# Query tiles of a PEER layer as fp16 pairs, and an even split of the gated expert columns

## The chip, the cores and the metric

The kernel runs on one core of a Trainium2 chip. The metric is the device time of one execution in microseconds, lower is better; where several runs were made, their median counts. The profile shows one execution, taken by the hardware profiler. Its engines are TensorE (PE; its weight loads are PEld), VectorE (DVE), ScalarE (ACT), GpSimd (POOL) and SyncE (SP), which issues most DMAs. L12 is line 12 of the kernel before.

## The reference

One decoder layer on 256 tokens of width 1024. An attention mixer (eight sparse-attention heads and four differential heads) comes first; the change doesn't touch it. Behind it stands a PEER layer, which is what this case is about:

```python
h = rmsnorm(x, norm2_g[l]) * (1 + sc_f) + sh_f
x = x + g_f * peer_ffn(h, peer_wq[l], peer_sub_keys[l], peer_u[l], peer_v[l])
return rmsnorm(x, final_g)

# peer_ffn, per chunk xc of 128 tokens
q = (xc @ wq).reshape(PEER_CHUNK, PEER_HEADS, 2, PEER_QDIM // 2)
sub = jnp.einsum('thpd,pkd->thpk', q, sub_keys)
sv, si = lax.top_k(sub, PEER_TOPK)
cand = sv[:, :, 0, :, None] + sv[:, :, 1, None, :]      # and the expert numbers cidx alike
best, pos = lax.top_k(cand, PEER_TOPK)
eid = jnp.take_along_axis(cidx, pos, axis=-1)
g = jax.nn.softmax(best, axis=-1)
act = jax.nn.gelu(jnp.einsum('td,thkd->thk', xc, u[eid]))
return jnp.einsum('thk,thkd->td', g * act, v[eid])
```

There are 8 heads, two halves of the query with 128 sub-keys each, 16 best per head, and 128 x 128 = 16,384 experts with a row of 1024 in `peer_u` and one in `peer_v`. A query tile is 128 columns of `wq`: 16 of them, two for each head.

## The kernel before

All 16,384 experts are computed densely. An expert's number is i * 128 + j; an expert tile j holds the 128 experts of one j, one to a partition. The layer runs in two loops of 128 steps, and a gating matrix, zero for all experts that a token did not choose, lies between them.

**The u loop** (`u_step`, L814). Step j loads 512 KB of `peer_u`, splits it into an fp16 pair (a scaled high part and the remainder, `split16`, L788: one operation of ScalarE at L793 and one of VectorE at L794), and makes three products for each of eight blocks of 128 features (`mm3`, L88 to L91): high times high, high times low, low times high. The 24 matmuls of 128x128 by 128x256 add up in one PSUM bank of pool `pu` (tile `up`, three buffers). ScalarE writes the gelu of the sum (L834) into the stash `st`, as 256 tokens of step j. The pair lies in one buffer of pool `hl` (tiles `w_hi` for even and `w_lo` for odd j, three buffers each). Loads and splits of expert tiles are traced with high priority.

**The range checks.** fp16 has a small range, so each split leaves a sum in a column of `chk`, and the first of each kind one in `big`. At the end `all_fit` (L1151) makes a flag of them, and if a number did not fit, a second version of the whole layer (fp32 pairs, from L1193) runs and writes the output again. Otherwise it is skipped.

**The choice of experts** (`topk_gen`, L856) is a generator that the u loop advances by a few steps after each expert tile (L1042). Heads 0 and 1 have their four query tiles from an earlier place (`qe`, L737 to L766, in fp32). For the other six heads, each of the two steps `wq` (L860) loads a query tile (`wraw`, a pool of its own with three buffers; the load has high priority) and multiplies it in fp32 with the fp32 input `h2` (L865). Two steps `sub_scores` (L869) multiply by the sub-keys `sk` (L873) and take the top 16 of each half with VectorE (`top16`, L849); a fifth step takes the top 16 of the sums. Two rounds of 14 steps then turn the choice into one-hot indices `kT` and weights `gT`, one round for 128 tokens. Where the steps and the loop's pace meet is at L1042: every second j before j = 12, then 2, 2, 1 steps in turn before j = 30, then one.

**Gating** (`g_build`, `g_apply`, `g_all`, L963 to L1008). For a group of eight tokens VectorE builds a one-hot A of the 128 i (L972) and a weighted one-hot of the j columns as two fp16 parts (B, Bl, L972 and L979); TensorE multiplies them (L988, two matmuls for each token, as wide as the j columns), and VectorE multiplies the result into the stash (L992). There are 32 groups of tokens, and two halves of the columns j: the first half (HJ = 72 columns, `st0`) is gated while the u loop goes on, as soon as the choice is done; the second (56 columns, `st1`) during the v loop. `paced` spreads the 65 steps of a half evenly, over the u steps that are left or over the first HJ - 6 v steps. Where u steps with j < 72 fall into the first half's gating, the expert tile is gated in part on the spot (L829 to L832, L994).

**The v loop** (`outputs`, L1049). Step j splits a 512 KB tile of `peer_v` and the gated stash row (tile `wt`, three buffers), and makes 12 matmuls of 128x128 by 128x512 (L1077) into four PSUM banks. Once the first HJ steps are past, the stash `st0` is scratch for the end of the kernel: final gains, inputs x (`xc`, L1101), modulation sums (`tail_prep`, L1106), one of its 20 pieces after each v step.

**Order and queues.** Within each engine instructions run in order. That order is made when the program is built: by priority, and by what an estimate says is ready. SP's queue carries the weight loads; ScalarE's queue carries the sub-keys (L842) and the store of `h2` (L843); POOL's queue carries the scratch loads (L1099, L1102, L1129, L1134).

Of the kernel before, what the change touches and what calls it, by code (L numbers as in the profile page):

```python
# [57 lines left out]
def block_kernel(ctx: ExitStack, tc: tile.TileContext, I, out):  # L58
# [50 lines left out]
    hchk = keep.tile([P, KD], F32, name="hchk")  # L109
    big = keep.tile([P, 3 + KD], F32, name="big")  # L110

# [642 lines left out]
    for k in range(KD):  # L754
        t = nrm[:, k % 2]
        V.tensor_mul(t, x2g[:, k, 0:T], rstd2)
        S.activation(h2[:, k], t, AF.Identity, bias=mod[:, 24 + k:25 + k])
        S.activation(h16[0][:, k], t, AF.Identity, bias=shs[:, k:k + 1], scale=SH, accum_out=big[:, 3 + k:4 + k])
        V.scalar_tensor_tensor(h16[1][:, k], h2[:, k], SH, h16[0][:, k], ALU.mult, ALU.subtract,
                               accum_out=hchk[:, k:k + 1])  # L760
# [21 lines left out]
    chk = keep2.tile([P, NCHK], F32, name="chk")  # L782
    G.memset(chk[:, 0:3 * NJ], 0.0)
    G.tensor_copy(chk[:, 3 * NJ:], hchk)
    first_one = {}
    bad_flag = keep2.tile([1, 1], I32, name="bad_flag")

    def split16(src, hi, lo, scale, i):  # L788
        kw = {}
        if i < 2 * NJ and i // NJ not in first_one:  # L790
            first_one[i // NJ] = i
            kw = dict(accum_out=big[:, 1 + i // NJ:2 + i // NJ])
        S.activation(hi, src, AF.Copy, scale=scale, **kw)  # L793
        V.scalar_tensor_tensor(lo, src, scale, hi, ALU.mult, ALU.subtract, accum_out=chk[:, i:i + 1])  # L794

    def load_split16(src, scale, i):
        with tc.high_priority(offset=None):
            t = load(src)
# [6 lines left out]
    pu = ps_u.enter_context(tc.tile_pool(name="pu", bufs=3, space=PSUM, reuse_waits="tile"))  # L805
    tk_stack = ExitStack()
    tk = tk_stack.enter_context(tc.tile_pool(name="tk", bufs=2, reuse_waits="tile"))
    tk1 = tk_stack.enter_context(tc.tile_pool(name="tk1", bufs=1, reuse_waits="tile"))

    act_box, hr_box = [], []  # L810
# [24 lines left out]

    iota_i = tk1.tile([P, P], I32, name="iota_i")
    G.iota(iota_i, pattern=[[1, P]], base=0, channel_multiplier=0)
    G.tensor_copy(iota, iota_i)
    c15 = tk1.tile([P, PH * TK], U32, name="c15")
    G.memset(c15, 15)  # L840
    sk = tk1.tile([P, 2, P], F32, name="sk")
    nc.scalar.dma_start(sk, I["peer_sub_keys"])  # L842
    nc.scalar.dma_start(h2d, h2)  # L843
    sv = tk1.tile([P, 2, 2, PH, TK], F32, name="sv")
    si = tk1.tile([P, 2, 2, PH, TK], U32, name="si")
    best = tk1.tile([P, 2, PH, TK], F32, name="best")
    bpos = tk1.tile([P, 2, PH, TK], U32, name="bpos")

    def top16(vals, tmp, vout, iout):  # L849
# [5 lines left out]

    def topk_gen():  # L856
        for h in range(PH):
            qs = {p: qe[:, 2 * h + p] for p in range(2)} if h < 2 else {}

            def wq(p):  # L860
                with tc.high_priority(offset=None):
                    w = load(I["peer_wq"][2 * h + p], pool=tk, name="wraw", bufs=3)
                ps = pu.tile([P, T], F32, name="up")
                for k in range(KD):
                    PE.matmul(ps, w[:, k * P:(k + 1) * P], h2[:, k], start=k == 0, stop=k == KD - 1)  # L865
                qs[p] = tk.tile([P, T], F32, name="qT")
                S.copy(qs[p], ps)

# [10 lines left out]

            for f, p in ((wq, 0), (wq, 1), (sub_scores, 0), (sub_scores, 1))[2 if h < 2 else 0:]:  # L880
                f(p)
                yield
# [141 lines left out]

    tg = topk_gen()
    alive = True
    gg = None
    for j in range(NJ):
        if not alive and gg is None:
            tk_stack.close()  # L1030
            st1_pool = ctx.enter_context(tc.tile_pool(name="stash1", bufs=1))
            st.append(st1_pool.tile([P, NJ - HJ, T], F32, name="st1"))
            act_stack = ExitStack()
            act_box.append(act_stack.enter_context(tc.tile_pool(name="actp", bufs=2)))
            h2_stack.close()
            gp_stack = ExitStack()
            gp_box.append(gp_stack.enter_context(tc.tile_pool(name="gp", bufs=2, side="right", reuse_waits="tile")))
            gg, first = g_all(0), j + 3
        u_step(j, True)
        done_j[0] = j + 1  # L1040
        if alive:
            alive = pump(tg, j % 2 if j < 12 else (2, 2, 1)[j % 3] if j < 30 else 1)  # L1042
        elif j >= first:
            paced(gg, j - first, NJ - 4 - first)
    ps_u.close()
    act_stack.close()
    w_pool = ctx.enter_context(tc.tile_pool(name="wp", bufs=LAST))

    def outputs(half, gg):  # L1049

        inner = ExitStack()
        py = inner.enter_context(tc.tile_pool(name="py", bufs=1, space=PSUM))
        if not half:
# [38 lines left out]
        def scratch(i, n=1):  # L1092
            return scr[:, i * D:(i + n) * D]
# [6 lines left out]
        xf = [scratch(4), scratch(5)]  # L1100
        xc = scratch(16, 2).rearrange("p (k t) -> p k t", k=KD)  # L1101
        nc.gpsimd.dma_start(xc, x2d)  # L1102
# [48 lines left out]
        def all_fit():  # L1151

            ok = scratch(2)[:, 0:NCHK]
            V.tensor_mul(ok, chk, chk)
            V.tensor_scalar(ok, ok, LIM * LIM, None, ALU.is_lt)
            V.tensor_mul(big[:, 1:], big[:, 1:], big[:, 1:])
            V.tensor_reduce(big[:, 0:1], ok, axis=AX.X, op=ALU.min)
            V.tensor_scalar_mul(big[:, 0:1], big[:, 0:1], LOW / (P - 0.5))
            ps = pg.tile([P, NT, P], F32, name="gps").rearrange("p a b -> p (a b)")[0:1, 0:3 + KD]
            PE.matmul(ps, ones[:, 0:1], big, start=True, stop=True)  # L1160
            small = scratch(2)[0:1, 0:3 + KD]
            V.tensor_scalar(small, ps, LOW, None, ALU.is_lt)
            V.tensor_reduce(bad_flag, small, axis=AX.X, op=ALU.max)
# [26 lines left out]
    outputs(True, g_all(1))  # L1190
    gp_stack.close()
    rv = nc.values_load(bad_flag, min_val=0, max_val=1)
    with tc.If(rv > 0):  # L1193

        again = ExitStack()
        pu = again.enter_context(tc.tile_pool(name="pu", bufs=2, space=PSUM))
# [16 lines left out]
        again.close()  # L1213
        outputs(False, None)


# [63 lines left out]
```

## Time and profile before

| | us |
|---|---|
| median of 3 runs (lowest, highest) | 971.66 (971.08, 974.53) |
| the profiled execution | 968.78 |
| its span | 967.0 |
| TensorE's granted clock, mean | 0.99 |
| mixer and the start of the layer | 0 to 202 |
| u loop | 202 to 603 |
| v loop | 603 to 948 |
| end | 948 to 967 |

The profiled execution lies 2.9 us below the median. In the page's 40 slices each digit is the busy share of 24 us in tenths (9 is 90% or more):

```profile
PE   5989997999999999999999999999999998999995
DVE  7978888788475799468988988799999988655664
ACT  4458874574333465554444445545444544555552
DMA  9978557686544356755555555655555669756631
```

The u loop begins in the ninth slice, the v loop at the end of the 25th. A row of the groups says: line, engine, operation, output and inputs by name, shapes, count, then busy time in us and the mean in ns of one, then the engine's idle time just before and what ended it. Matmuls overlap each other, so the mean of one matmul is longer than its share of the time.

### The profile page before, as it was taken

What the parts mean: (1) busy time and instruction counts of PE and PEld (TensorE: products, weight loads), DVE (VectorE), ACT (ScalarE), POOL (GpSimd) and SP (SyncE); (2) the same over time, 40 slices, a digit from 0 to 9 for tenths busy, and PEclk for the clock granted to TensorE, in tenths of its full rate; (3) what the DMA queues carried; (4) which work ended last, traced back from release to release, by engine and by line L of the source; (5) the groups of instructions that cost most, each with busy time, mean ns of one, the idle gap of its engine ahead of it and who ended that gap; (6) DMA issues with size and microseconds to landing.
All of it is one profiled execution on the core that took longest, in us unless ns stands there. A gap on an engine that the chain in (4) does not pass through costs nothing.

```text
span 967.0 us, 18674 instructions
## 1 busy us (share of the span) xinstructions
PE 927.8 (96%) x7118; PEld 681.8 (71%) x7118; DVE 765.9 (79%) x2033; ACT 496.2 (51%) x901; POOL 14.5 (2%) x27
## 2 busy tenths in 40 slices
PE   5989997999999999999999999999999998999995
PEld 3987877888888888899999998444544543554442
DVE  7978888788475799468988988799999988655664
ACT  4458874574333465554444445545444544555552
POOL 0000010000000000000000000000000000000001
PEclk9999998999999999999999999999999999999998
DMA  9978557686544356755555555655555669756631
GB/s 361 357 296 267 156 176 239 236 293 190 181 156 155 123 176 200 234 195 184 177 189 181 178 192 177 217 198 181 191 193 182 214 218 331 233 177 198 212 112 48
DMA packets 54132, 197.55 MB, mean 204 GB/s; under 512 B 6145, under 2 KB 6417, under 8 KB 53522
## 3 DMA queue, kind: packets, MB, share of 16 engines
q1 hardware_dynamic: 52706, 191.38, 59.2%
q0 software_dynamic: 608, 3.17, 1.0%
q10 hardware_dynamic: 720, 1.74, 0.5%
q8 instruction: 57, 0.93, 0.4%
q14 instruction: 41, 0.34, 0.1%
HBM read 193.11 MB, written 3.15 MB: 203 GB/s over the span
## 4 chain that ended last, share of the span: by engine, by line
PE 85%; DVE 6%; DMA 4%; ACT 3%; issue 2%; SPq 0%; DVEq 0%; ACTq 0%
PE y L1077 28%; PE up L89 11%; PE up L90 11%; PE up L91 11%; PE up L865 4%; PE gps L988 3%; DMA raw<-in_ada_w_dram 2%; PE lg L350 2%; PE mm L90 1%; PE mm L91 1%; PE mm L89 1%; PE o L524 1%; DMA raw<-in_w_inK_dram 1%; PE gps L873 1%; DVE w_hi L794 1%
## 5 line engine op out<-in xcount | busy, mean ns | idle before, releaser
L1077 PEld LDWEIGHTS <-wt 128*128 128x128 f16 x1500 | 144.0, 98 | 170.3 <-DVE wt L794 5.1
L793 ACT ACTIVATE w_lo<-raw 128x1024 f16<-128x1024 f32 x128 | 135.2, 1057 | 173.7 <-PE y L1077 84.3
L793 ACT ACTIVATE w_hi<-raw 128x1024 f16<-128x1024 f32 x128 | 135.2, 1056 | 170.2 <-PE up L91 85.8
L794 DVE SCALAR_TENSOR_TENSOR w_lo<-raw,w_lo 128x1024 f16<-128x1024 f32 x128 | 156.3, 1221 | 62.9 <-ACT w_lo L793 60.5
L794 DVE SCALAR_TENSOR_TENSOR w_hi<-raw,w_hi 128x1024 f16<-128x1024 f32 x128 | 156.1, 1219 | 54.9 <-ACT w_hi L793 54.6
L1077 PE MATMUL y<-w_hi,wt 128*128 128x512 f16 x756 | 174.0, 379 | 2.0 <-DVE wt L794 2.0
L1077 PE MATMUL y<-w_lo,wt 128*128 128x512 f16 x744 | 171.0, 379 | 0.5 <-DVE wt L794 0.4
L89 PE MATMUL up<-h,w_hi 128*128 128x256 f16 x512 | 139.6, 273 | 2.1 <-ACT bq L765 2.1
L91 PE MATMUL up<-h,w_hi 128*128 128x256 f16 x512 | 139.6, 273 | 0.0
L90 PE MATMUL up<-h,w_hi 128*128 128x256 f16 x512 | 139.6, 273 | 0.0
L89 PE MATMUL up<-h,w_lo 128*128 128x256 f16 x504 | 137.4, 273 | 0.0
L91 PE MATMUL up<-h,w_lo 128*128 128x256 f16 x504 | 137.4, 273 | 0.0
L90 PE MATMUL up<-h,w_lo 128*128 128x256 f16 x504 | 137.4, 273 | 0.0
L794 DVE SCALAR_TENSOR_TENSOR wt<-st,wt 128x256 f16<-128x256 f32 x128 | 53.6, 419 | 4.7 <-ACT wt L793 4.7
L90 PEld LDWEIGHTS <-w_hi 128*128 128x128 f16 x512 | 50.1, 98 | 8.2 <-issue 2.3
L793 ACT ACTIVATE wt<-st 128x256 f16<-128x256 f32 x128 | 51.3, 401 | 7.6 <-PE y L1077 5.6
L90 PEld LDWEIGHTS <-w_lo 128*128 128x128 f16 x512 | 50.1, 98 | 6.1
L91 PEld LDWEIGHTS <-w_hi 128*128 128x128 f16 x512 | 50.1, 98 | 5.8
L91 PEld LDWEIGHTS <-w_lo 128*128 128x128 f16 x512 | 50.0, 98 | 5.8
L89 PEld LDWEIGHTS <-w_lo 128*128 128x128 f16 x512 | 50.1, 98 | 5.7
L89 PEld LDWEIGHTS <-w_hi 128*128 128x128 f16 x512 | 50.2, 98 | 5.5
L972 DVE TENSOR_TENSOR B<-iota,kT 128x576 f16<-128x576 f16 (+1 forms) x64 | 27.1, 424 | 28.9 <-PE gps L988 28.8
(366 smaller groups left out, 1489.2 us busy)
## 6 DMA issues: line engine op xcount, KB each, us to landing
raw<-in_peer_u_dram SPq DMA_DIRECT2D x128, 512.0 KB, 3.5
raw<-in_peer_v_dram SPq DMA_DIRECT2D x128, 512.0 KB, 3.8
adal<-in_ada_w_dram SPq DMA_DIRECT2D x24, 512.0 KB, 4.5
adaw<-in_ada_w_dram SPq DMA_DIRECT2D x16, 512.0 KB, 5.5
raw<-in_w_inK_dram SPq DMA_DIRECT2D x16, 512.0 KB, 7.4
wraw<-in_peer_wq_dram SPq DMA_DIRECT2D x12, 512.0 KB, 4.3
raw<-in_cmp_w_dram SPq DMA_DIRECT2D x8, 512.0 KB, 4.4
raw<-in_w_out_dram SPq DMA_DIRECT2D x8, 512.0 KB, 4.4
```

What stands on the lines that cost most here:

```text
L89: PE.matmul(ps, w[0], m[0], start=start, stop=False)
L90: PE.matmul(ps, w[0], m[1], start=False, stop=False)
L91: PE.matmul(ps, w[1], m[0], start=False, stop=stop)
L350: PE.matmul(out, q[x][pr, ts], rhs, start=i == 0, stop=i == 2)
L524: PE.matmul(o[:, h * 64:(h + 1) * 64], pt[:, h * P:(h + 1) * P], vst[sb][:, b, g], start=False, stop=bi == len(blocks) - 1 and h == 3)
L793: S.activation(hi, src, AF.Copy, scale=scale, **kw)
L794: V.scalar_tensor_tensor(lo, src, scale, hi, ALU.mult, ALU.subtract, accum_out=chk[:, i:i + 1])
L865: PE.matmul(ps, w[:, k * P:(k + 1) * P], h2[:, k], start=k == 0, stop=k == KD - 1)
L873: PE.matmul(sps[:, t], qs[p][:, t * P:(t + 1) * P], sk[:, p], start=True, stop=True)
L972: V.tensor_tensor(pairs(x), io, kT[:, i, t0:t0 + NT, None, :].to_broadcast(four), ALU.is_equal)
L988: PE.matmul(ps[:, q, 0:n], A[:, q], Bg[i][:, q], start=i == 0, stop=i == 1)
L1077: PE.matmul(yps[t][n], w[:, ts], m[:, ns], start=j == 0 and first, stop=j == NJ - 1 and last)
```

## The change

Four things change together.

1. The twelve query tiles of heads 2 to 7 are split into fp16 pairs by `load_split16`, with high priority, in the buffers of the expert tiles, and multiplied by `mm3` with the fp16 pair of the input. Each leaves a range check (12 more columns of `chk` in use, one more of `big`).
2. The choice of experts is now a part of the repeated version: `topk_gen` makes its own tiles in its first step and takes the input and the early queries as arguments; without the latter it works in fp32 throughout. So `h2` is read back there, and some pools close earlier.
3. HJ is 64 in place of 72: both halves of the gating have 64 columns, and the second half is spread over 58 v steps in place of 66. `xc` moves within the scratch.
4. The pace of the choice: from j = 12 to 35 two steps after every fourth expert tile and one after the others; from 36 on two after every sixth. The choice ends at j = 60 in place of 58, and gating of the first half starts at step 64 in place of 62. The store of `h2` is issued ahead of the load of the sub-keys in the program's text.

```diff
-    HJ = 72
+    HJ = 64
...
-    NCHK = 3 * NJ + KD
+    NCHK = 3 * NJ + 2 * PH + KD
...
     def split16(src, hi, lo, scale, i):
         kw = {}
-        if i < 2 * NJ and i // NJ not in first_one:
-            first_one[i // NJ] = i
-            kw = dict(accum_out=big[:, 1 + i // NJ:2 + i // NJ])
+        kind = 2 if i < 0 else i // NJ
+        if i < 2 * NJ and kind not in first_one:
+            first_one[kind] = i
+            kw = dict(accum_out=big[:, 1 + kind:2 + kind])
+        if i < 0:
+            i += NCHK - KD
         S.activation(hi, src, AF.Copy, scale=scale, **kw)
         V.scalar_tensor_tensor(lo, src, scale, hi, ALU.mult, ALU.subtract, accum_out=chk[:, i:i + 1])
...
-    nc.scalar.dma_start(sk, I["peer_sub_keys"])
-    nc.scalar.dma_start(h2d, h2)
...
-    def topk_gen():
+    def topk_gen(pools, pu, h2, qe):
...
+        nc.scalar.dma_start(sk, I["peer_sub_keys"])
...
+        yield
         for h in range(PH):
...
             def wq(p):
-                with tc.high_priority(offset=None):
-                    w = load(I["peer_wq"][2 * h + p], pool=tk, name="wraw", bufs=3)
-                ps = pu.tile([P, T], F32, name="up")
-                for k in range(KD):
-                    PE.matmul(ps, w[:, k * P:(k + 1) * P], h2[:, k], start=k == 0, stop=k == KD - 1)
+                i = 2 * h + p
                 qs[p] = tk.tile([P, T], F32, name="qT")
-                S.copy(qs[p], ps)
+                kw = dict(pool=tk, name="wraw", bufs=3)
+                if qe is not None:
+                    hi, lo = load_split16(I["peer_wq"][i], SU, i - 2 * PH, **kw)
+                    ps = pu.tile([P, T], F32, name="up")
+                    for k in range(KD):
+                        c = slice(k * P, (k + 1) * P)
+                        mm3(ps, (hi[:, c], lo[:, c]), (h16[0][:, k], h16[1][:, k]), k == 0, k == KD - 1)
+                    S.activation(qs[p], ps, AF.Copy, scale=1.0 / (SU * SH))
+                else:
...
-    tg = topk_gen()
-    alive = True
+    nc.scalar.dma_start(h2d, h2)
+    tk_stack = ExitStack()
+    tg = topk_gen(tk_stack, pu, h2, qe)
+    alive = pump(tg, 1)
...
-            alive = pump(tg, j % 2 if j < 12 else (2, 2, 1)[j % 3] if j < 30 else 1)
+            alive = pump(tg, j % 2 if j < 12 else 2 if j % (4 if j < 36 else 6) == 0 else 1)
...
-        xc = scratch(16, 2).rearrange("p (k t) -> p k t", k=KD)
+        xc = scratch(8, 2).rearrange("p (k t) -> p k t", k=KD)
...
     rv = nc.values_load(bad_flag, min_val=0, max_val=1)
     with tc.If(rv > 0):
+        again = ExitStack()
+        pu = again.enter_context(tc.tile_pool(name="pu", bufs=2, space=PSUM))
+        h2 = again.enter_context(tc.tile_pool(name="h2p", bufs=1, side="right")).tile([P, KD, T], F32, name="h2")
+        nc.sync.dma_start(h2, h2d)
+        for _ in topk_gen(again, pu, h2, None):
+            pass
+        again.close()
```

More of the change, by code (lines that the diff above doesn't have):

```diff
@@ L109, in block_kernel @@
     hchk = keep.tile([P, KD], F32, name="hchk")
-    big = keep.tile([P, 3 + KD], F32, name="big")
+    big = keep.tile([P, 4 + KD], F32, name="big")
     ph1 = ExitStack()
@@ L857, in topk_gen @@
         for h in range(PH):
-            qs = {p: qe[:, 2 * h + p] for p in range(2)} if h < 2 else {}
+            qs = {p: qe[:, 2 * h + p] for p in range(2)} if qe is not None and h < 2 else {}
             def wq(p):
-                with tc.high_priority(offset=None):
-                    w = load(I["peer_wq"][2 * h + p], pool=tk, name="wraw", bufs=3)
-                ps = pu.tile([P, T], F32, name="up")
-                for k in range(KD):
-                    PE.matmul(ps, w[:, k * P:(k + 1) * P], h2[:, k], start=k == 0, stop=k == KD - 1)
-                qs[p] = tk.tile([P, T], F32, name="qT")
-                S.copy(qs[p], ps)
+                i = 2 * h + p
+                qs[p] = tk.tile([P, T], F32, name="qT")
+                kw = dict(pool=tk, name="wraw", bufs=3)
[7 more added lines that the diff above has]
+                else:
+                    w = load(I["peer_wq"][i], **kw)
+                    ps = pu.tile([P, T], F32, name="up")
+                    for k in range(KD):
+                        PE.matmul(ps, w[:, k * P:(k + 1) * P], h2[:, k], start=k == 0, stop=k == KD - 1)
+                    S.copy(qs[p], ps)
@@ L1030, in block_kernel @@
             tk_stack.close()
-            st1_pool = ctx.enter_context(tc.tile_pool(name="stash1", bufs=1))
+            st1_pool = late.enter_context(tc.tile_pool(name="stash1", bufs=1))
             st.append(st1_pool.tile([P, NJ - HJ, T], F32, name="st1"))
@@ L1158, in all_fit @@
             V.tensor_scalar_mul(big[:, 0:1], big[:, 0:1], LOW / (P - 0.5))
-            ps = pg.tile([P, NT, P], F32, name="gps").rearrange("p a b -> p (a b)")[0:1, 0:3 + KD]
+            ps = pg.tile([P, NT, P], F32, name="gps").rearrange("p a b -> p (a b)")[0:1, 0:4 + KD]
             PE.matmul(ps, ones[:, 0:1], big, start=True, stop=True)
-            small = scratch(2)[0:1, 0:3 + KD]
+            small = scratch(2)[0:1, 0:4 + KD]
             V.tensor_scalar(small, ps, LOW, None, ALU.is_lt)
@@ L1191, in block_kernel @@
     gp_stack.close()
+    late.close()
     rv = nc.values_load(bad_flag, min_val=0, max_val=1)
     with tc.If(rv > 0):
+        again = ExitStack()
[5 more added lines that the diff above has]
+        again.close()
+        late = ExitStack()
+        st[1] = late.enter_context(tc.tile_pool(name="stash1", bufs=1)).tile([P, NJ - HJ, T], F32, name="st1")
         again = ExitStack()
@@ L1214, in block_kernel @@
         outputs(False, None)
+        late.close()
 def bias_rows(rel_bias):
```

40 lines of the change are left out of this document (20 added, 20 removed).

## The prediction

> **What bounds the kernel now.** I read the page's totals and its chain first, then busy time by stretch, then what TensorE waits for.
>
> ```profile
> PE 927.8 (96%) x7118; PEld 681.8 (71%) x7118; DVE 765.9 (79%) x2033; ACT 496.2 (51%) x901; POOL 14.5 (2%) x27
> PE 85%; DVE 6%; DMA 4%; ACT 3%; issue 2%; SPq 0%; DVEq 0%; ACTq 0%
> ```
> ```profile
> 237.00:331.00 94.00, 94.00 (x675) 83.63 (x674) 60.46 (x324) 31.61 (x60) 0.00 (x0) 1.00 0.47 157
> 406.00:603.00 197.00, 197.00 (x2166) 178.19 (x2165) 164.19 (x311) 93.40 (x151) 0.00 (x0) 1.00 0.55 183
> 603.00:762.00 159.00, 159.00 (x1112) 78.19 (x1111) 143.20 (x359) 77.69 (x114) 1.10 (x2) 1.00 0.61 198
> 762.00:820.00 58.00, 55.64 (x341) 25.78 (x337) 50.92 (x125) 28.82 (x42) 1.09 (x2) 1.00 0.77 260
> 202.00:603.00 401.00, 400.85 (x3842) 360.45 (x3842) 316.88 (x910) 187.42 (x314) 0.00 (x0) 1.00 0.56 185
> 603.00:948.00 345.00, 342.54 (x2054) 164.61 (x2053) 269.44 (x678) 173.07 (x262) 2.19 (x4) 1.00 0.62 201
> PE y L1077 <- DVE wt L794: 2.4, 4, 1.2
> PE up L89 <- ACT bq L765: 2.1, 1, 2.1
> ```
> The columns of a stretch are its length, then the busy time of PE, PEld, DVE, ACT and POOL, the granted clock, the DMA share and GB/s. From 202 to 948 us TensorE is busy 743.4 of 746 us, at full clock, and in that time it waits 2.4 us for another engine (the last two rows). So a matmul taken out of this part shortens the run one for one, as long as VectorE, ScalarE and the transfers still arrive in time. The expert loop ("u", 401 us) and the output loop ("v", 345 us) are both TensorE's. VectorE is the runner-up: 64% busy while the query tiles are made (237 to 331), 83% while the first half is gated, and 90% in the first 159 us of v.
>
> **The change part by part.** *Query tiles.* In fp32 two of them stand together in the chain of waits, and an expert tile's 24 fp16 matmuls lie between the starts of two tiles:
>
> ```profile
> L865 PE MATMUL up<-h,wraw 128*128 128x256 f32 x192 | 42.4, 379 | 0.0
> 238.16 6.91 PE up L865 x32
> 247.69 0.89 PE gps L873 x8
> 202.16 0.27 PE L89 MATMUL up<-h,w_hi 128*128 128x256 f16 x1 [2.07 <-ACT bq L765]
> 204.77 0.27 PE L89 MATMUL up<-h,w_lo 128*128 128x256 f16 x1
> ```
> The 379 ns is a pipelined latency, so the price comes from starts. 6.91/32 is 216 ns a record, 16 records a tile, 192 in all: 41.46 us. An expert tile takes 204.77 - 202.16 = 2.61 us. A query tile becomes the same 24 matmuls, so twelve cost 31.32 us. TensorE's saving is **10.1 us**.
>
> The new work beside it is a split per tile, on the two engines that already split the expert tiles:
>
> ```profile
> L793 ACT ACTIVATE w_hi<-raw 128x1024 f16<-128x1024 f32 x128 | 135.2, 1056 | 170.2 <-PE up L91 85.8
> L794 DVE SCALAR_TENSOR_TENSOR w_hi<-raw,w_hi 128x1024 f16<-128x1024 f32 x128 | 156.1, 1219 | 54.9 <-ACT w_hi L793 54.6
> ACT qT L867 <- PE up L865: 31.5, 12, 3.1
> ```
> That is 12 x 1.06 = 12.7 us on ScalarE and 12 x 1.22 = 14.6 us on VectorE. The twelve copies to qT become activations of the same shape, priced the same. The new pace gives each of the six heads four expert tiles (two query tiles behind the first of them), 24 in all in place of 18. The stage is then 24 x 2.61 + 31.3 + 6 x 0.89 = 99 us. VectorE has 60.5 + 14.6 + 6 x 1.22 = 82 us of work in it (83%), ScalarE about 53 us. TensorE still covers both, so I price the splits at nothing. In the second row ScalarE's 31.5 us of waiting for fp32 matmuls also say that it has room. If that cover went, each uncovered split would cost up to 2.3 us (a rival below).
>
> *Gating, 72/56 to 64/64 columns.* TensorE's gating matmuls, 16 to a group of eight tokens, by starts:
>
> ```profile
> 424.56 0.52 PE gps L988 x16
> 761.85 0.19 PE L988 MATMUL gps<-B,A 128*128 128x56 f16 x1
> 762.27 2.75 PE L1077 MATMUL y<-w_lo,wt 128*128 128x512 f16 x12
> 830.20 2.59 PE y L1077 x12
> ```
> A 72-wide one takes 0.52/16 = 32.5 ns, a 56-wide one 0.42/16 = 26.3 ns. The 64-wide one stands in no row; between these ends I take the middle, 29.4 ns. Before: 512 x 32.5 + 512 x 26.3 = 30.1 us. After: 1024 x 29.4 = 30.1 us. **0**, bounds -3.2 (all at 26.3) and +3.2 (all at 32.5).
> [...]
>
> VectorE's share moves from u to v. One 56-wide group costs the sum of these forms, one 72-wide group likewise:
>
> ```profile
> L972 DVE TENSOR_TENSOR A<-iota,kT 128x1024 f16<-128x1024 f16 x64 | 43.8, 685 | 0.0
> L992 DVE TENSOR_TENSOR st<-gps,st 128x576 f32<-128x576 f32 x29 | 21.7, 750 | 0.0
> L992 DVE TENSOR_TENSOR st<-gps,st 128x448 f32<-128x448 f32 x32 | 19.7, 617 | 0.0
> L979 DVE TENSOR_TENSOR B<-B,gT 128x576 f16<-128x576 f16 x32 | 14.6, 458 | 1.1
> L972 DVE TENSOR_TENSOR B<-iota,kT 128x448 f16<-128x448 f16 x32 | 12.5, 391 | 8.6 <-PE gps L988 8.5
> ```
> With three B operations per group, 56-wide is 0.69 + 3 x 0.39 + 0.62 = 2.48 us and 72-wide 0.69 + 3 x 0.46 + 0.75 = 2.82 us; 64-wide lies between, 2.65, 7% over 56. These durations overlap a little, so I scale what the v stretch shows. Its 159 us hold 26 groups and 57 v steps and 143.2 us of busy VectorE, of which 26 x 2.48 = 64.5 of a sum of 169, or 38%, is gating: 54.6 us, 2.10 per group, and 88.6/57 = 1.55 per step for the rest. After the change 32 groups lie in 58 steps (HJ - 6) in place of 66: 1.55 + 0.55 x 2.10 x 1.07 = 2.79 us a step. TensorE needs 2.59 + 0.55 x 16 x 0.0294 = 2.85. So VectorE goes from 90% to **98%** there, and I take **0**; with 72-wide prices it would be 2.86, over the line by a hair. In u, gating gets lighter; the few partial operations of expert columns 64 to 71 go, off the path.
>
> *What moves in queues.* The sub-key load (L842) is now written behind the 1 MB store of h2 (L843) on ScalarE's queue, and its reader stands early in TensorE's order:
>
> ```profile
> 186.66 0.34 ACTq L842 DMA_DIRECT2D sk<-in_peer_sub_keys_dram  x1
> 202.14 0.34 ACTq L843 DMA_DIRECT2D h2d<-h  x1
> h2d<-h ACTq DMA_DIRECT2D x1, 1024.0 KB, 10.3
> sk<-in_peer_sub_keys_dram ACTq DMA_DIRECT2D x1, 128.0 KB, 4.0
> 207.39 0.61 PE L873 MATMUL gps<-sk,qe 128*128 128x128 f32 x4
> 754.87 0.54 POOL L1129 DMA_DIRECT2D st<-in_c_dram  x1 [133.37 <-DVE B L979]
> 768.02 0.55 POOL L1134 DMA_DIRECT2D st<-in_rows_dram  x1 [12.61 <-DVE wt L794]
> 801.57 0.54 POOL L1102 DMA_DIRECT2D st<-x2d  x1 [33.00 <-DVE wt L794]
> ```
> If the written order held, sk would leave at 202.5 and land between 206.5 and 216.8 (202.5 + 10.3 + 4.0), and L873 at 207.4, with every expert matmul behind it, would wait 0 to 9.4 us. I take 0: the store cannot leave before h2 exists at 202, and POOL's rows show L1129 and L1134 ahead of L1102, which is written before both, so queues are filled by readiness. The x copy (L1102) moves to scratch rows that come free earlier; it is late-bound today and nobody waits.
>
> *End.* The check reads 408 columns for 392 at L1154, L1155 and L1157 (about 0.5 us each): +0.05 us. The repeated half is skipped.
>
> **Sum:** 968.78 - 10.1 + 0 + 0 + 0.05 = **958.7 us** against the profiled execution. The median of the runs shown is 2.9 us above it, so **961.6** on the median's scale.
>
> **The rivals.** (1) *VectorE takes over the first 58 v steps.* At 98% it has no spare for the stretch after it, where eight 1.22 us modulation sums join, with waits for their loads:
>
> ```profile
> L1109 DVE CUSTOM_DVE_ANT_0 raw<-raw,st 128x1024 f32<-128x1024 f32 x8 | 9.8, 1225 | 6.6 <-DMA raw<-in_ada_w_dram 6.4
> DVE B L972 <- PE gps L988: 7.6, 25, 0.3
> ```
> Against: in 603 to 762 VectorE itself waits 7.6 us for gating matmuls, so it is ahead of TensorE, up to the three buffers of split tiles. For: if it enters the sums without that lead, up to 3 x 2.59 = 7.8 us go on top of today's 2.4, and 58 x 0.01 to 0.02 before. Result 962 to 971.
>
> (2) *Slower: split query tiles hold the buffers of the expert tiles.* The splits are now urgent like the loads, and the loads run far ahead:
>
> ```profile
> 178.18 1.43 SPq L69 DMA_DIRECT2D wraw<-in_peer_wq_dram  x3
> ```
> Three query tiles are loaded 60 us before their first use at 238. Split that early, they would take three of the six shared w_hi/w_lo buffers until used, and one name would be left with one. An expert tile of that name could then start its split only when the one two before it is used: 1.06 + 1.22 = 2.28 us in the 2.61 us of the other name's tile. Top-k work ahead on VectorE (blocks of about 2.5 us) would come on top: up to 2.2 us for each of 18 such tiles among the first 36, 39 us. It decides from 0.83 us a tile, 15 us in all; in the middle, 25 us, 986 us. Against: TensorE's order is also made by readiness, and a query tile that is ready in a gap would be used there and free its buffer.
>
> (3) *64-wide gating costs what 56-wide does.* Then 3.2 us more go: 958.4. [...]
>
> (4) *The sub-keys land late* (above): up to 9.4 us back, 971.
>
> (5) *It doesn't do what it says: a range check fails and the repeated half runs.* It repeats u and v at no less than today's 401 + 345 us: over 1700. The query weights are split with the scale that serves the expert weights, so this is remote.
>
> **How the numbers follow.** My forecast's chance is 0.56. (1) has 0.20, two thirds of it below 966.7; (2) 0.10; (3) 0.06; (4) 0.07; (5) 0.01. The measurement tells about 0.5% (4.9 us) from no change. Faster by more: 0.56 + 0.06 + 0.13 + 0.01 of (4) = 0.76. Within: 0.07 + 0.06 = 0.13. Slower: 0.11. The range reaches from (3) to the ends of (1) and (4), 957.5 to 971: that leaves out (2), (5) and a little at both ends, under 0.2.
>
> **What would show it.** Right: no fp32 matmuls on tile up; 288 more of L89 to L91; u about 391 us long; TensorE's waits in v under 4 us; VectorE near 98% up to the end of gating and its waits for gps almost gone; sk issued near 187. Wrong: TensorE waiting for VectorE's wt or w_lo between 600 and 800 (1); splits of query tiles before 202 and TensorE waiting on w_hi in the first expert steps (2); TensorE waiting at L873 (4). The number is most exposed where the order of VectorE's work is made anew by the change.

## The result, and the profile after

The changed kernel takes 955.91 us (median of 4 runs, 954.33 to 956.96) against 971.5 (971.08 to 974.53): 0.9834 of the time before, 95% interval 0.9821 to 0.9847. Its profiled execution took 955.93 us. Forecast were 961.6 us within 957.5 to 971.0: the sign was right, and the gain was half as large again as forecast and outside the range.

The totals and the chain of the changed kernel, then its busy time by stretch (length, then PE, PEld, DVE, ACT, POOL, the granted clock, DMA share, GB/s):

```profile
PE 918.5 (96%) x7214; PEld 675.4 (71%) x7214; DVE 777.0 (81%) x2051; ACT 509.5 (53%) x907; POOL 14.5 (2%) x27
PE 90%; DVE 3%; ACT 3%; DMA 2%; issue 1%; SPq 0%; ACTq 0%; DVEq 0%
```
```profile
203.80:593.00 389.20, 389.20 (x3938) 351.04 (x3938) 325.57 (x928) 200.71 (x317) 0.00 (x0) 1.00 0.59 191
593.00:750.00 157.00, 157.00 (x1133) 78.77 (x1132) 147.37 (x364) 75.29 (x111) 1.64 (x3) 1.00 0.62 199
750.00:800.00 50.00, 49.98 (x275) 23.45 (x273) 45.57 (x111) 26.58 (x40) 0.55 (x1) 1.00 0.81 285
```
TensorE holds 90% of the chain in place of 85%. VectorE is busier (94% in 593 to 750, where 98% was forecast), and TensorE is busy in all of 203.8 to 750 us. The waits from 203 to 948 us in the changed kernel say the same (engine, tile and line, what ended the wait; us, times, longest):

```profile
DVE B L984 <- PE gps L1000: 24.2, 43, 0.7
PE up L89 <- ACT bq L765: 2.1, 1, 2.1
DVE raw L1123 <- DMA raw<-in_ada_w_dram: 1.0, 1, 1.0
PE gps L1174 <- DVE big L1172: 0.2, 1, 0.2
```
The two rows of before that this answers to are `PE y <- DVE wt` (2.4 us), which is gone, and VectorE's wait for modulation weights, 6.4 us there and 1.0 us here.

To place the gain, I cut every profiled execution at three rows of its timeline. In the changed kernel:

```profile
203.76 0.27 PE L89 MATMUL up<-h,w_hi 128*128 128x256 f16 x1 [2.06 <-ACT bq L765]
593.45 0.81 PE L1091 MATMUL y<-w_hi,wt 128*128 128x512 f16 x3
937.03 0.58 DVE L1168 TENSOR_TENSOR st<-chk 128x408 f32<-128x408 f32 x1
```
The *start* lasts to the first expert matmul, the *expert loop* to the first output matmul, the *output loop* to the range check, the *end* to the span's end (954.0). All runs of the study:

| run | us (median) | ratio, 95% interval | start | expert loop | output loop | end |
|---|---|---|---|---|---|---|
| before | 971.5 | | 202.16 | 401.32 | 345.00 | 18.52 |
| aa (before again) | 971.53 | 0.9989 (0.9976, 1.0003) | 204.99 | 401.32 | 345.81 | 18.58 |
| changed kernel | 955.91 | 0.9834 (0.9821, 0.9847) | 203.76 | 389.69 | 343.58 | 16.97 |
| aa_after (again) | 957.25 | 0.9853 (0.9838, 0.9868) | 204.28 | 389.69 | 343.39 | 16.94 |
| q_only | 960.5 | 0.9878 (0.9856, 0.99) | 203.90 | 391.31 | 344.78 | 18.71 |
| hj_only | 969.05 | 0.9968 (0.9955, 0.9981) | 206.47 | 399.63 | 343.40 | 18.30 |
| pace_only | 971.69 | 0.9992 (0.9978, 1.0007) | 204.09 | 401.42 | 346.81 | 18.38 |
| q_half | 961.63 | 0.9903 (0.9884, 0.9922) | 201.84 | 394.70 | 343.39 | 16.97 |
| no_pairs | 968.84 | 0.997 (0.9958, 0.9982) | 205.90 | 401.37 | 343.60 | 16.93 |
| scr_load | 967.28 | 0.9953 (0.9939, 0.9968) | 205.74 | 401.32 | 341.87 | 17.87 |
| cond_late | 973.38 | 1.0012 (1.0002, 1.0022) | 205.94 | 401.32 | 346.32 | 18.62 |
| cond_early | 957.83 | 0.986 (0.9844, 0.9875) | 204.32 | 389.69 | 344.26 | 16.93 |
| scr_both | 955.81 | 0.9841 (0.9823, 0.9859) | 203.33 | 389.68 | 343.39 | 17.00 |
| no_redo | 959.37 | 0.9879 (0.986, 0.9899) | 205.48 | 389.69 | 344.06 | 18.47 |
| no_block | 968.85 | 0.9969 (0.9957, 0.998) | 205.28 | 401.32 | 344.52 | 15.38 |
| pad_dve | 971.57 | 1.0 (0.9988, 1.0013) | 205.45 | 401.33 | 346.18 | 18.34 |
| pad_dve100 | 969.45 (one run) | | 202.53 | 401.33 | 345.23 | 18.61 |
| pad_pe | 970.79 (one run) | | 203.87 | 401.33 | 345.53 | 18.27 |
| pad_act | 972.25 | 1.0009 (0.9999, 1.0019) | 205.81 | 401.32 | 346.53 | 18.54 |
| pad_queues | 970.52 (one run) | | 204.52 | 401.32 | 345.97 | 16.89 |

The start varies from 202 to 206 us whatever the kernel; the other three stages repeat. The expert loop gives 11.63 us and the end 1.6. The output loop of before takes 345.75 us as the mean of seven profiles whose running work is the kernel before's (before, aa and the five pad runs; 345.0 to 346.5), and 343.4 to 343.6 in the changed kernel: 2.2 us. Together 15.4, against 15.6 between the medians.

### The profile page after: what moved, and what is told of

It reads as the page before. It is cut to its first block, busy times and chain, and to the rows that moved or that the text cites. A ratio compares the mean times of both kernels' runs of the same rounds, so it can differ in the third digit from the quotient of the medians.

```text
span 954.0 us, 18893 instructions
## 1 busy us (share of the span) xinstructions
PE 918.5 (96%) x7214; PEld 675.4 (71%) x7214; DVE 777.0 (81%) x2051; ACT 509.5 (53%) x907; POOL 14.5 (2%) x27
## 4 chain that ended last, share of the span: by engine, by line
PE 90%; DVE 3%; ACT 3%; DMA 2%; issue 1%; SPq 0%; ACTq 0%; DVEq 0%
PE y L1091 34%; PE up L89 13%; PE up L90 13%; PE up L91 13%; PE gps L1000 3%; PE lg L350 2%; PE mm L90 1%; PE mm L91 1%; PE mm L89 1%; DMA raw<-in_w_inK_dram 1%; PE o L524 1%; PE tr L89 1%; PE tr L90 1%; PE gps L885 1%; PE tr L91 1%
## 5 line engine op out<-in xcount | busy, mean ns | idle before, releaser
L89 PE MATMUL up<-h,w_hi 128*128 128x256 f16 x560 | 152.6, 273 | 2.1 <-ACT bq L765 2.1
L90 PE MATMUL up<-h,w_hi 128*128 128x256 f16 x560 | 152.6, 273 | 0.0
L91 PE MATMUL up<-h,w_hi 128*128 128x256 f16 x560 | 152.6, 273 | 0.0
L89 PE MATMUL up<-h,w_lo 128*128 128x256 f16 x552 | 150.5, 273 | 0.0
L91 PE MATMUL up<-h,w_lo 128*128 128x256 f16 x552 | 150.5, 273 | 0.0
L90 PE MATMUL up<-h,w_lo 128*128 128x256 f16 x552 | 150.5, 273 | 0.0
L90 PEld LDWEIGHTS <-w_hi 128*128 128x128 f16 x560 | 54.8, 98 | 8.5 <-issue 2.3
L90 PEld LDWEIGHTS <-w_lo 128*128 128x128 f16 x560 | 54.8, 98 | 6.3 <-issue 0.2
L91 PEld LDWEIGHTS <-w_lo 128*128 128x128 f16 x560 | 54.8, 98 | 6.3
L91 PEld LDWEIGHTS <-w_hi 128*128 128x128 f16 x560 | 54.8, 98 | 6.3
L89 PEld LDWEIGHTS <-w_lo 128*128 128x128 f16 x560 | 54.8, 98 | 6.1
L89 PEld LDWEIGHTS <-w_hi 128*128 128x128 f16 x560 | 54.8, 98 | 6.1
L984 DVE TENSOR_TENSOR B<-iota,kT 128x512 f16<-128x512 f16 x64 | 27.1, 423 | 24.4 <-PE gps L1000 24.2
```

The costliest lines, as they stand in the source:

```text
L89: PE.matmul(ps, w[0], m[0], start=start, stop=False)
L90: PE.matmul(ps, w[0], m[1], start=False, stop=False)
L91: PE.matmul(ps, w[1], m[0], start=False, stop=stop)
L984: V.tensor_tensor(pairs(x), io, kT[:, i, t0:t0 + NT, None, :].to_broadcast(four), ALU.is_equal)
```

## The experiments: the parts alone

**aa, the kernel before once more**, to know what two profiles of one kernel differ by.

> The kernel before, unchanged, profiled again. It asks how far the profiled execution on record (968.78 us, 2.7 us under the median of its kernel) is typical. If the offset is chance: time within 0.3% of the kernel before, and a new profile with u near 401.4 us and v near 344.8 us, in which any other length lies in the start (0 to 202 us) or the end (18.5 us). If the offset is a stall in v that varies: v differs by 2 us or more between the two profiles.

The expert loop repeats to 0.01 us, the output loop to 0.8. The start came 2.8 us later than in the execution from which I predicted.

**q_only, the fp16 pairs alone** (72 columns, the old pace, the choice of experts where it was).

```diff
-                    w = load(I["peer_wq"][2 * h + p], pool=tk, name="wraw", bufs=3)
...
-                    PE.matmul(ps, w[:, k * P:(k + 1) * P], h2[:, k], start=k == 0, stop=k == KD - 1)
...
-                S.copy(qs[p], ps)
+                hi, lo = load_split16(I["peer_wq"][i], SU, i - 2 * PH, pool=tk, name="wraw", bufs=3)
...
+                    mm3(ps, (hi[:, c], lo[:, c]), (h16[0][:, k], h16[1][:, k]), k == 0, k == KD - 1)
+                S.activation(qs[p], ps, AF.Copy, scale=1.0 / (SU * SH))
```

> Kernel before with only the twelve query tiles as fp16 pairs (HJ 72, old pace; the repeated half, which is skipped, keeps the first choice of experts). Price-per-matmul theory: u 10.1 us shorter, v as before with TensorE waiting about 2.4 us for wt, time about 961.4 us, ratio 0.9896. Rival, that the splits need the new pace as cover: TensorE waits for w_hi or w_lo in u, gain under 8 us.

The expert loop fell by 10.01 us; the output loop and the end stayed as before. The pairs give what the count of matmuls says and nothing else.

**hj_only, 64 columns alone, and pace_only, the new pace alone.**

```diff
-    HJ = 72
+    HJ = 64
...
-        xc = scratch(16, 2).rearrange("p (k t) -> p k t", k=KD)
+        xc = scratch(8, 2).rearrange("p (k t) -> p k t", k=KD)
```

> Kernel before with HJ 64 for 72 (and xc in other scratch rows), nothing else. Theory now, from the two traces: u 1.6 us shorter (narrower gating matmuls), v 1.6 us longer for the wider ones but 3.0 us shorter because the wait in the modulation sums goes: in all 3.0 us, ratio 0.9969. The prediction on record said 0 for this part: ratio 1.000.

```diff
-            alive = pump(tg, j % 2 if j < 12 else (2, 2, 1)[j % 3] if j < 30 else 1)
+            alive = pump(tg, j % 2 if j < 12 else 2 if j % (4 if j < 36 else 6) == 0 else 1)
```

> Kernel before with only the new pace of the choice of experts. Both theories: TensorE has the same matmuls and no wait in u, so 0, ratio within 0.1% of 1. If the pace is worth something by itself, u is shorter by over 1 us.

The pace does nothing that can be measured. The 64 columns, with the copy `xc` in other rows, which the prediction had at zero together, give 0.32% alone: 1.69 us of the expert loop, where gating got narrower, and, in the output loop, where it got wider, a gain too. This is the surprise of the study. The narrower half itself is right: in the changed kernel's chain a group's sixteen 64-wide matmuls stand as

```profile
421.48 0.47 PE gps L1000 x16
427.19 0.47 PE gps L1000 x16
```
or 29.4 ns each, the value assumed; 512 of them in place of 512 at 32.5 ns are 1.6 us less in the expert loop, and 512 in place of 512 at 26.3 ns are 1.6 us more in the output loop. So the output loop gave up 1.6 us and still ended shorter.

**q_half, half of the pairs undone in the changed kernel** (heads 5 to 7 in fp32 again).

```diff
-                if qe is not None:
+                if qe is not None and h < 5:
                     hi, lo = load_split16(I["peer_wq"][i], SU, i - 2 * PH, **kw)
```

> The changed kernel with the last six of the twelve query tiles (heads 5 to 7) in fp32 again in the first pass. Theory: each query tile as a pair is worth (41.46 - 31.32)/12 = 0.845 us of TensorE's time in the expert loop with full cover, so six of them cost 5.07 us: expert loop 389.69 + 5.07 = 394.8 us, output loop unchanged, time 961 us. Rival: part of the gain is a wait that goes (splits, buffers) and not the matmuls' own time; then the six tiles cost less or more than 5.07 by over 0.5 us.

389.69 became 394.70: 5.01 us for six tiles, 0.835 each. The gain follows the number of matmuls; no wait is hidden in it.

## The experiments: the stall behind the gating

Behind the gating of the second half stand the eight modulation sums, each with a 512 KB load. In aa, the chain of waits from 781 to 821 us holds four of these loads one after another (start, us, what):

```profile
784.60 3.13 DMA raw<-in_ada_w_dram
789.02 5.80 DMA raw<-in_ada_w_dram
797.37 4.51 DMA raw<-in_ada_w_dram
807.16 8.07 DMA raw<-in_ada_w_dram
```
and its waits from 203 to 948 us say who stands behind them:

```profile
DVE raw L1109 <- DMA raw<-in_ada_w_dram: 7.3, 4, 3.2
PE y L1077 <- DVE wt L794: 3.0, 4, 2.1
```
While VectorE waits for a load, the split of the next stash row (`wt`) stands behind it in VectorE's order, and TensorE waits for that. Issue and first sum in the timelines, of the kernel before and then of the changed one:

```profile
781.76 0.33 SPq L69 DMA_DIRECT2D raw<-in_ada_w_dram  x1
785.64 1.23 DVE L1109 CUSTOM_DVE_ANT_0 raw<-raw,st 128x1024 f32<-128x1024 f32 x1 [0.86 <-DMA raw<-in_ada_w_dram]
```
```profile
751.99 0.33 SPq L69 DMA_DIRECT2D raw<-in_ada_w_dram  x1
764.88 1.22 DVE L1123 CUSTOM_DVE_ANT_0 raw<-raw,st 128x1024 f32<-128x1024 f32 x1
```
Before, the load has 3.9 us until its sum; after, 12.9. In the instruction orders of the two kernels the first of these loads leaves behind the 73rd output tile's load before and behind the 65th after, eight steps earlier, since the loop that issues them begins at step HJ. The sums come only five to six steps earlier (the first with step 62 for 67): their other input, the vector `cond2`, lies in stash rows that come free at the same step in both. So in the order of the instructions each load has gained about three steps of 2.6 us. In time only the first two show it: the other six have 4.0 to 6.6 us until their sums in the changed kernel, and 4.7 to 7.5 before, with the waiting itself in that figure. What does differ is how many sums wait: six of eight before (6.4 us), one after (1.0 us).

A first rival: VectorE is simply overloaded where the sums meet the last gating groups, and 64 columns, ending earlier, part the two. Four runs bear on it. A second rival, which no run was made for, is the 1 MB copy of x; it follows behind cond_early.

**scr_load, the kernel before with these loads in free stash rows**, issued some 40 steps earlier.

```diff
-                w = load(I["ada_w"][ct])
+                w = scratch(2 + ct - 40)
+                nc.sync.dma_start(w, I["ada_w"][ct])
```

> Kernel before with the eight modulation tiles loaded straight into freed stash rows, some forty steps early, nothing else; the sums then stand at steps 64 to 72, in the middle of gating (last at 68). If the loads' lateness cost the 3 us: no wait of VectorE for in_ada_w, none of TensorE for wt, v about 341.9 us for 345.0, ratio 0.996. Rival, that it is VectorE's load, gating and sums together: TensorE still waits 2 us or more for wt, v near 345, ratio 1.000.

The output loop fell to 341.87, VectorE has no row for this wait any more and TensorE none for `wt`, and the chain of this run from 765 to 830 us goes through TensorE alone:

```profile
791.39 0.86 PE y L1077 x4
792.26 0.01 issue
792.27 37.94 PE y L1077 x175
```
The stall was thus worth 345.75 - 341.87 = 3.9 us on average, 3.1 in the execution from which I predicted (scr_load was profiled once). With the 1.6 us of wider gating on top, 341.87 becomes 343.5, which is what the changed kernel takes.

**cond_late, the kernel before with the sums' vector in rows that come free later**, so that the sums begin behind the gating.

```diff
-        ada_b2 = scratch(15)[:, 0:48]
+        ada_b2 = scratch(13)[:, 0:48]
...
-        cond2 = scratch(13)
+        cond2 = scratch(15)
```

> Kernel before with cond2 in stash rows that come free eight steps later; the sums start at step 68 for 67, two of them one step later, all behind the end of gating (68). Late loads: the sums still follow their loads closely, VectorE waits 4 us or more for them, TensorE about 2 us, v 344 to 345.5 us. Rival, gating and sums together: with the overlap gone no wait, v 341.9 us.

Its waits from 203 to 948 us:

```profile
DVE raw L1109 <- DMA raw<-in_ada_w_dram: 5.2, 4, 3.2
PE y L1077 <- DVE wt L794: 3.4, 3, 2.2
```
Sums and gating hardly overlap any more (first sum with step 68, and of the gating only the last product into the stash, 2.3 us behind it), and the stall stays. In aa too all of VectorE's waits for these loads lie behind the last gating product. The overload theory falls; the loads stand.

**cond_early, the changed kernel with that vector in rows that come free early** (ready at step 17 for 61), so that the sums can move up to their loads.

```diff
-        cond2 = scratch(13)
+        cond2 = scratch(2)
...
-        th2 = scratch(14)
+        th2 = scratch(3)
```

> Changed kernel with the conditioning vector of the modulation sums (cond2) in stash rows that come free 44 steps earlier, nothing else. VectorE's order then has the eight sums at v steps 59 to 68, three steps nearer to their loads than in the changed kernel (62 to 70). If the wait for the loads was what cost TensorE 3 us before: VectorE waits 5 us or more for in_ada_w again, TensorE waits 2.4 to 4 us for wt, v about 346.5 us for 343.6, ratio to the kernel before 0.987. Rival, that a lighter v loop saved it: no wait returns, ratio 0.984.

In large part a miss. The sums moved up three steps, and some of VectorE's wait came back:

```profile
DVE raw L1123 <- DMA raw<-in_ada_w_dram: 3.5, 5, 1.1
```
but in pieces of at most 1.1 us; TensorE has no wait for `wt`, where 2.4 to 4 us were expected, and the output loop grew by only 0.7 to 0.9 us, hardly more than the 0.5 to 0.7 of no_redo below, whose running work is the changed kernel's. Yet here the first load leaves six tiles ahead of the step of its sum (65 and 59), as in the kernel before (73 and 67), and two gating products come behind the first sum, as before. So the lateness of the loads alone doesn't make the stall of before.

**The second rival: the copy of x.** Part 3 of the change also moves `xc` in the scratch, and with it POOL's 1 MB copy of x. With 72 columns it leaves 198 us into the output loop, amid the eight loads; with 64 it leaves 108 us into it, long before them. In aa, and then in the changed kernel:

```profile
805.03 0.54 POOL L1102 DMA_DIRECT2D st<-x2d  x1 [33.62 <-DVE wt L794]
812.22 1.23 DVE L1109 CUSTOM_DVE_ANT_0 raw<-raw,st 128x1024 f32<-128x1024 f32 x1 [3.24 <-DMA raw<-in_ada_w_dram]
815.00 1.90 PE L1077 MATMUL y<-w_hi,wt 128*128 128x512 f16 x8 [2.10 <-DVE wt L794]
```
```profile
701.49 0.54 POOL L1116 DMA_DIRECT2D st<-x2d  x1 [90.58 <-DVE wt L798]
```
The copy takes 9.1 us in aa, and the two loads that share that time take about 8 us each (8.07 is the last of the four above; the first took 3.13). VectorE's longest wait, 3.2 of its 7.3 us, is for one of them, and TensorE's longest, 2.1 of 3.0, stands behind it. cond_late and the pad runs show the same (longest waits of 3.2 and 2.2 us in cond_late, a copy of 7.7 to 8.6 us in pad_dve, pad_dve100 and pad_pe); in the execution from which I predicted the copy takes 7.4 us and the share is smaller (VectorE 1.6 of 6.4, TensorE about 1.1 of 2.4). No run moved the copy alone. So it is shown that the wait for these loads is the stall; how much of its end is due to their earlier place and how much to the copy's is open.

**scr_both, the edit of scr_load in the changed kernel** (rows 2, 3, 7, 10, 11, 4, 5, 6).

> The changed kernel with the eight tiles of modulation weights loaded into free stash rows instead of the pool of the expert tiles, as the same edit of the kernel before that took its output loop from 345 to 341.9 us. There the stall of the sums went (about 3 us). Theory: in the changed kernel no such stall is left on TensorE, so the edit can only take the rest of VectorE's waits (0.7 us) away: output loop 343 to 343.6 us, time within 0.5 us of the changed kernel. Rival: loads of 512 KB more room for the tiles of the output loop help by themselves; then the output loop shortens by over 1 us here too.

Nothing: 343.39, and 0.9841 beside 0.9834 and 0.9853. The changed kernel has no stall left for it, so the change and this edit take the same 3 to 4 us.

## The experiments: the end

The end is 1.6 us shorter in the changed kernel, and its recorded work isn't: the last output is issued 11.5 us after the range check begins, in both (948.57 - 937.03 and 959.98 - 948.48). The difference lies behind it, where no engine records work. What moves there are instruction fetches. For the kernel before, the DMA rate from 960.4 us to its end in 40 slices of 0.165 us, and the instruction queue (packets, MB, share):

```profile
GB/s 99 372 397 385 385 348 410 385 335 124 99 62 12 12 0 0 0 0 0 50 0 0 0 0 0 99 0 0 0 0 0 0 0 50 0 0 0 0 0 0
q14 instruction: 7, 0.06, 2.7%
```
The left part is the last output. The lone 50 (and 99) are one (and two) packets of 8 KB in a slice: three fetch times, 1.0 and 1.3 us apart, and the end 1.1 us after the last. In the changed kernel, from 948.9 us on in slices of 0.128 us, there are six packets, the last three 0.6 and 0.4 us apart, and the end follows 0.6 us after the last:

```profile
GB/s 0 112 321 418 402 386 337 370 402 369 337 402 209 80 96 32 16 16 0 0 0 0 0 0 0 0 0 64 0 0 0 0 64 0 0 64 0 0 0 0
q14 instruction: 6, 0.05, 2.5%
```

**aa_after, no_pairs, no_redo: whose end is it?** aa_after is the changed kernel again; no_pairs has the query tiles in fp32 in the first pass, no_redo no choice of experts in the skipped block.

```diff
-                if qe is not None:
+                if False:
```
```diff
     with tc.If(rv > 0):
-        again = ExitStack()
...
-        for _ in topk_gen(again, pu, h2, None):
-            pass
-        again.close()
```

> The changed kernel, unchanged, profiled again. Its end (from the range check to the last instruction) was 17.0 us, 1.3 to 1.7 us shorter than in five other kernels. If that belongs to its program: 17.0 again. If it is chance: 18.3 to 18.7. u 389.7 and v 343.5 us either way.

> The changed kernel with the twelve query tiles computed in fp32 again in the first pass (one column of the early range check is set to a constant in their place). Everything else stays: the choice of experts in the repeated block, 64 columns, the new pace. Theory: the pairs are worth 10.0 us of the expert loop and nothing elsewhere, so the expert loop takes 389.7 + 10.0 = 399.7 us, as in the kernel before with 64 columns alone; the output loop stays at 343.4 to 343.6; the time is 955.9 + 10 = 966. The end tells two theories apart: if the short end (16.9 us) comes from the choice of experts in the skipped block, it stays 16.9; if it comes from the pairs' splits and their range checks, it is 18.3 to 18.7 again and the time is 967.5.

> The changed kernel without the choice of experts in the repeated block, which is skipped in these runs: the block would use the first pass's choice, as the kernel before does. Not one instruction that runs is taken away. Theory of the short end: the program of each engine behind the skipping branch decides how long the end takes; then the end is 18.3 to 18.7 us again in place of 16.9 and the time goes up by 1.4 to 1.8 us, to 957.3 to 957.7. Rival: the end belongs to the pairs or the 64 columns; then it stays at 16.9 and the time within 0.5 us of the changed kernel. Expert loop 389.7, output loop 343.4 to 343.6 by both.

Without the pairs 16.93, without the choice in the skipped block 18.47: the short end hangs on instructions that never run. no_redo's other stages stayed, but for half a us of the output loop. no_pairs missed in another place: its expert loop was 401.37 in place of 399.7. The granted clock accounts for it. In its timeline TensorE's wait ahead of the loop was longer than elsewhere, and the stretches behind it show what followed:

```profile
205.90 0.27 PE L89 MATMUL up<-h,w_hi 128*128 128x256 f16 x1 [3.26 <-ACT bq L765]
```
```profile
204.00:207.10 3.10, 1.20 (x12) 1.07 (x12) 3.10 (x7) 3.07 (x9) 0.00 (x0) 1.00 1.02 336
207.20:210.60 3.40, 3.40 (x19) 2.40 (x17) 0.54 (x4) 1.25 (x4) 0.19 (x1) 0.50 0.98 352
210.60:214.00 3.40, 3.40 (x32) 3.10 (x31) 1.23 (x2) 3.10 (x5) 0.00 (x0) 0.99 0.97 361
```
For 3.4 us the granted clock was 0.50, which costs 1.7 us: 399.63 (hj_only) + 1.7 = 401.3. That this run's median is no better than hj_only's fits a dip in many of its executions; only one was profiled.

**no_block, the kernel before without the jump and the block** (the range check is still computed, nothing reads it; the fp32 fallback is left out).

```diff
-    rv = nc.values_load(bad_flag, min_val=0, max_val=1)
-    with tc.If(rv > 0):
...
```

> The kernel before without the branch and without the repeated block behind it (the range check is still computed, nothing reads it). Theory: after the last output of the kernel before, engines jump over the block and the rest of the program is fetched in 3 to 4 steps one after another, about 1.2 us each; without the jump what follows is fetched ahead, as in the rest of the program, so that only the landing of the last output (about 2.3 us) and the finish are left: the end takes 14 to 15.5 us in place of 18.5, time 967.5 to 969. Rival: those 5 to 7 us after the last issue belong to the end of any program; then the end is 16.9 to 18.7 here too.

An end of 15.38 us and 0.31% less time, and behind the last output one fetch in place of seven, about 1.7 us behind the end of the span:

```profile
q8 instruction: 1, 0.02, 0.5%
```
So the jump and the block cost the kernel before 3.1 us by the spans. In this execution 2.6 us of its time lie outside the span, in that of before 1.8; with these added the difference is 2.3 us, and between the medians it is 3.0. The changed kernel wasn't run without its block; by the spans its end is 1.6 us above 15.38.

**pad_dve, pad_dve100, pad_pe, pad_act, pad_queues: which engine's program?** Each adds instructions to the skipped block of the kernel before, of one engine or of two: in this order pad_dve (100 in place of 312 in pad_dve100), pad_pe, pad_act and pad_queues.

```diff
     with tc.If(rv > 0):
+        for _ in range(312):
+            V.memset(bad_flag, 0)
```
```diff
     with tc.If(rv > 0):
...
+        for _ in range(300):
+            PE.matmul(pps, ident, ident, start=True, stop=True)
...
```
```diff
     with tc.If(rv > 0):
+        for _ in range(42):
+            S.copy(hchk[:, 0:1], hchk[:, 1:2])
```
```diff
     with tc.If(rv > 0):
+        for _ in range(18):
+            nc.sync.dma_start(hchk, I["rows"][:, 0:KD])
+        for _ in range(3):
+            G.memset(hchk[:, 0:1], 0.0)
```

> The kernel before with 312 small VectorE writes put into the repeated block, which is skipped; nothing that runs is changed. The changed kernel's block holds some 306 rows of VectorE more than before. Theory: the length of VectorE's skipped program sets how the end is fetched behind the jump, so the end falls from 18.3-18.7 to about 16.95 us and the fetches of instructions after the last output from 7 to 6; time 970.0. Rival: another engine's program sets it; then the end stays at 18.3 to 18.7. Expert loop 401.3, output loop 345 to 346.8 by both.

> The same with 100 such writes. If the place where VectorE's program goes on (its position modulo a unit of fetching) decides, the end can fall on either side, 16.95 or 18.5 us, and differ from the run with 312; if only the block's length counts, with a threshold between 0 and 306 rows, it is 18.5 below and 16.95 above. If VectorE doesn't set it, 18.3 to 18.7.

> The kernel before with 300 small TensorE matmuls (and their weight loads) in the skipped block. By the theory that VectorE's program decides the end stays at 18.3 to 18.7 us; by the rival that TensorE's does, it falls to 16.95 us.

> The kernel before with 42 small ScalarE copies put into the skipped block, so that ScalarE jumps over as many instructions as in the changed kernel (581 in place of 539). ScalarE is the last engine that reaches the jump. Theory: ScalarE's program decides how many fetches follow one after another, so the end falls from 18.3-18.7 to about 16.95 us and 6 fetches in place of 7 follow the last output; time 970. Rival: GpSimd's or SyncE's program decides it, or the sum of all; then 18.3 to 18.7. Expert loop 401.3, output loop 345 to 346.8 by both.

> The kernel before with 18 small loads on SyncE's queue and 3 small writes of GpSimd in the skipped block, about what the choice of experts adds there in the changed kernel. If SyncE's or GpSimd's program decides the end, it is 16.95 us; if ScalarE's does, 18.3 to 18.7.

My two theories, VectorE's program (18.34 and 18.61) and then ScalarE's (18.54), fell, and so did the rival, TensorE's (18.27): all three leave the end where it was. 18 loads and 3 small writes on SyncE's and GpSimd's programs bring 16.89, in one execution, and six packets behind the last output:

```profile
q14 instruction: 6, 0.05, 1.5%
```
So it is one of these two programs, or both. Which it is, and whether the length of the block or the place of what follows it decides, wasn't tried. That the fetches are what the end waits for is read from their times and number, not shown by a run.

## Why the prediction was wrong

**Query tiles, right.** 10.14 us forecast; 10.01 measured alone, 5.01 for half. The 288 more matmuls of L89 to L91 are there (w_hi 512 to 560, w_lo 504 to 552 per line in the groups of the two kernels), the fp32 ones on `up` are gone, and their splits cost nothing, as priced. The forecast expert loop was about 391 us; it is 389.69.

**Gating's own price, right.** Zero in sum, as +1.6 and -1.6. The rival that 64 columns cost what 56 do falls: 29.4 ns lies on the line from 26.3 (56 columns) to 32.5 (72).

**The failed step: "up to 3 x 2.59 = 7.8 us go on top of today's 2.4".** I took the stall behind the gating as a floor, to which a fuller VectorE could only add, and priced the move of HJ by the operations that it makes wider or narrower. The stall was there to be won: 3.1 us in the execution that I read and 3.9 on average, so the output loop was forecast at 1.6 us longer and came out 2.2 shorter. What the move of HJ also moves are the eight loads, eight steps earlier on SP's queue, while their readers moved five to six, and the copy of x, some 90 us earlier in the output loop. I had quoted both waits (VectorE's 6.4 us for these loads, TensorE's 2.4) and never asked when the loads are issued, and of the copy I wrote "it is late-bound today and nobody waits", where in aa VectorE's longest wait is for a load that runs beside it. That the wait for the loads was the stall is shown by scr_load; which of the two moves ended it stays open. That TensorE's row said 2.4 where 3.1 were lost has its reason in the view: a matmul of L1077 is drawn 379 ns long and takes 216 (2.59 us for twelve), so that small gaps vanish in its length: 0.16 us in each of the four waits makes 0.65.

**"The repeated half is skipped."** The jump over it isn't free: the end was to grow by 0.05 us and shrank by 1.6. On the scale of the medians the two misses are 3.8 + 1.6 = 5.4 of the 5.7 us between forecast and result. Adding 2.9 us for the median was sound: the execution that I read had an early start (202.16; 204.99 when profiled again).

**The rivals.** VectorE did not take over: 94% busy, not 98, and its waits for gating matmuls, which were to be almost gone, are 4.7 us in 593 to 750, where the same stretch before had 7.6:

```profile
DVE B L984 <- PE gps L1000: 4.7, 15, 0.4
```
So its price of 2.79 us a step was too high (94% of TensorE's 2.85 are 2.68), without effect on the sum. The splits of query tiles did not run ahead and hold buffers, and the sub-keys were not late; in the changed kernel's timeline of ScalarE's work and queue:

```profile
188.27 0.34 ACTq L854 DMA_DIRECT2D sk<-in_peer_sub_keys_dram  x1
225.81 1.06 ACT L797 ACTIVATE w_lo<-wraw 128x1024 f16<-128x1024 f32 x1 [1.29 <-PE up L91]
```
The first split of a query tile runs at 225.8, not before 202, and the sub-keys leave at 188 although they are written behind the store of `h2`, which leaves at 203.9: the order by readiness held. The repeated half did not run.

## What to carry to other kernels

When a loop bound moves, ask of every transfer behind it when its buffer comes free, when its reader runs, and which other transfers run then; a load that lands late stalls what stands behind its reader (in aa VectorE waited 7.3 us for such loads and TensorE 3.0 for the split behind them), and that wait is there to be won as well as lost. A small wait in the profile is a candidate for gain, not a floor: follow it to the issue row of its transfer before pricing a change around it. Code that is jumped over can still have a price at the jump, 2.3 to 3.1 us in the kernel before, and it can move when only the skipped part changes.

## What the hardware showed unexpectedly

- In the kernel before, the jump and the block that never runs cost 2.3 to 3.1 us, and the number of instruction fetches behind the last output went with the end: 15.4 us without the jump and one fetch, behind the end of the span (no_block), 18.3 to 18.6 us with it and seven fetches (before, aa and four of the pad runs), 16.9 us with 21 more skipped instructions on two engines and six (pad_queues). The last three fetch times stand 1.0 and 1.3 us apart in the kernel before and 0.6 and 0.4 in the changed one; that the end waits for these fetches is my reading of such rows, and no run shows it.
- In no_pairs a wait of TensorE of 3.3 us was followed by 3.4 us at clock 0.50; waits of 2.1 us at the same place in before, hj_only, no_redo and the changed kernel were followed by clock 1.00. Only one execution shows the dip: that the wait brought it, and how long such a wait has to be, was not shown.
